# Down projection of a gated FFN, taken product by product over all channel pairs, with the block sums made earlier and kept in DRAM

## The chip, the cores and the metric

One core of one Trainium2 chip runs the whole kernel. The metric is device time in microseconds, the median of several runs. A profiled execution of the same program gives the trace; its times are microseconds from the start of the span unless marked ns. PE is TensorE's matmul, PEld its weight load, DVE VectorE, ACT ScalarE, POOL GpSimd, SP the engine whose queue issues most DMAs.

## What is computed

A decoder block on a sequence of 1024 tokens with 1024 channels, in float32: input projections, two kinds of token mixing, an output projection, and then a gated feed-forward part. The last part matters here:

```python
h = rmsnorm(x, norm2_g)
u = h @ w_ffn_up                      # 1024 x 5632
a, b = u[..., :D_FF], u[..., D_FF:]   # D_FF = 2816
a = causal_dwconv(a, ffn_conv_w, ffn_conv_b)
x = x + (jax.nn.silu(a) * b) @ w_ffn_down
return rmsnorm(x, norm_f_g)
```

## The kernel before

**Precision.** A float32 product is made of three matmuls (`mm3`, L206 to L209). Each operand is split (`split`, L194 to L196) into a high half, rounded by an ACT copy (L195), and a low half, the difference, made by DVE or, for the weights of the input projections, by POOL (L196).

**Seven products.** The up and the down projection use a Strassen-like scheme: both operands of a 2x2 block product are cut into four blocks, and seven block products take the place of eight. `left` (L1245) and `right` (L1261) make the sums and differences of blocks that a product needs, in place, on POOL mostly (`add` and `sub`, L1240 and L1243), and split them.

**Order.** The program is written in Python order, and a scheduler orders each engine's instructions by written order and by when it reckons them ready; the order in the trace is therefore not the written one everywhere. Tiles of one tag share a fixed number of buffers: `slab` and `sl2` (four each, 16 KB per partition), `raw` and `rw` (two each, for raw weights), `w4` and `op` (four each, operands), `f4` (four), and four PSUM tags of two banks.

**Early stage.** The values and gates of the mLSTM part are projected token tile by token tile (`vgates`, L283), then `gates()` (L312) makes the gate rows in two slabs, and 22 input projections follow (`project`, L400; `pweights`, L386, loads and splits one projection's weights into `w4` tiles). Each projection calls `tick()` twice (L377), which advances the generators in `active`, among them the mLSTM chunks.

**Up stage** (L1280 to L1389). For each of the 22 channel tiles f the loop loads four weight blocks, makes products 1 and 2 (`first_up`, L1322) and then 5, 6, 7, 3 and 4 (`rest_up`, L1341). A product is one PSUM bank, 12 matmuls. The convolution, the SiLU and the gating (`conv_up`, `gate_up`, L1330 and L1336) give the gated tile, two halves of 512 tokens, which are stored to `d_g` in DRAM.

**Down stage** (L1392 to L1500). Two channel tiles make a pair, 11 pairs in all. The pairs are taken in four groups of 2, 2, 3 and 4 (`GROUPS`). A pair's gated blocks and weight blocks are loaded once, 2 MB (`load_down`). Within a group all seven products are made one after the other (`prod_down`, L1428): it makes each pair's left and right sum, splits both, multiplies four token tiles into four PSUM banks, and adds each bank to a running tile in `X` (L1445, L1240). In the last group the running tiles are combined (`acc`) and rows are finished (`finish`, L1456): squares, root, scaling and the store of the output.

## Time and profile before

| | |
|---|---|
| median of 3 runs | 1388.04 us (1385.54 to 1392.6) |
| the profiled execution's own time | 1398.64 us |
| its span, first to last instruction | 1396.8 us |
| TensorE busy, of the span | 92% |
| DVE busy, of the span | 78% |
| ACT and POOL busy, of the span | 39% each |
| mean granted TensorE clock | 0.956 of full speed |

Busy shares are means over stages with different limits. The stages in the trace: gate projections and input projections to about 400 us, the token mixing to about 700, the up stage to 1133.5, the down stage to the end. A view of busy time over stretches of time shows which engine is full in which stage; the view of waits says what ended an idle time; the view of lines gives the mean duration of each kind of instruction.

### The profile page before, as it was taken

To read this page: it belongs to the slowest core of one execution; us is meant where nothing else is said; L and a number is where in the kernel's file an instruction comes from. 1 tells how busy PE (TensorE), PEld (TensorE's weight loads), DVE (VectorE), ACT (ScalarE), POOL (GpSimd) and SP (SyncE) were. 2 spreads that over 40 slices of the span, in tenths; PEclk is the share of its full clock that TensorE was granted. 3 is DMA by queue.
4 is the path that set the end of the run, shared out by engine and by line. 5 is a ranking of instruction groups with operands and counts; after the bars stand their busy time and mean duration, and the time that the engine had idled before them with its cause. 6 is when DMAs were issued, how large, how long until landed. Compare 5 with 4: busy or idle time off the path is not lost.

```text
span 1396.8 us, 20908 instructions
## 1 busy us (share of the span) xinstructions
PE 1285.8 (92%) x7814; PEld 1028.4 (74%) x7814; DVE 1084.9 (78%) x1777; ACT 540.4 (39%) x969; POOL 543.1 (39%) x379
## 2 busy tenths in 40 slices
PE   5999999888978889999989999999999999989794
PEld 5978777666767767677768888888888888768563
DVE  6376874898762786667599888787777878999998
ACT  6343334662211333223353434333333345434234
POOL 4102112534231334221464444333443365573971
PEclk9999999998995889899999999999999999999997
DMA  6111332365552664434324222222222293312003
GB/s 223 46 40 49 103 87 59 109 171 142 149 152 71 173 184 131 130 108 131 122 80 161 91 91 91 91 79 72 76 92 91 76 344 123 121 38 84 0 0 121
DMA packets 126549, 150.19 MB, mean 108 GB/s; under 512 B 49384, under 2 KB 88168, under 8 KB 126448
## 3 DMA queue, kind: packets, MB, share of 16 engines
q1 hardware_dynamic: 115568, 135.74, 30.9%
q10 hardware_dynamic: 10880, 13.11, 3.3%
q8 instruction: 62, 1.02, 0.3%
q14 instruction: 39, 0.32, 0.1%
HBM read 108.41 MB, written 40.40 MB: 107 GB/s over the span
## 4 chain that ended last, share of the span: by engine, by line
PE 59%; DVE 26%; issue 4%; ACT 4%; DMA 4%; POOL 2%; SPq 0%; DVEq 0%; ACTq 0%; POOLq 0%
PE ps L207 17%; PE ps L208 16%; PE ps L209 16%; DVE op L196 6%; DVE slab L196 2%; DVE slab L1240 2%; DVE sl L1240 2%; DVE slab L704 1%; PE ps L942 1%; DVE slab L702 1%; DMA d_x<-raw 1%; DVE w L273 1%; PE ps L1056 1%; DVE sv L606 1%; PE ps L1018 1%
## 5 line engine op out<-in xcount | busy, mean ns | idle before, releaser
L207 PE MATMUL ps<-sl,w 128*128 128x512 f32 x416 | 172.0, 414 | 0.0
L208 PE MATMUL ps<-sl,w 128*128 128x512 f32 x416 | 168.2, 404 | 1.2 <-POOL w L196 1.2
L209 PE MATMUL ps<-sl,w 128*128 128x512 f32 x416 | 168.4, 405 | 0.0
L207 PE MATMUL ps<-slab,op 128*128 128x512 f32 x388 | 156.4, 404 | 7.4 <-DVE slab L196 6.6
L1243 POOL TENSOR_TENSOR raw<-raw,rw 128x512 f32<-128x512 f32 x44 | 85.5, 1943 | 187.0 <-DVE op L196 181.0
L208 PE MATMUL ps<-slab,op 128*128 128x512 f32 x388 | 154.7, 399 | 2.8 <-DVE op L196 2.8
L209 PE MATMUL ps<-slab,op 128*128 128x512 f32 x388 | 154.8, 399 | 0.0
L196 POOL TENSOR_TENSOR w<-raw,w 128x1024 fp32r<-128x1024 f32 x22 | 54.1, 2459 | 209.1 <-ACT w L195 171.0
L207 PE MATMUL ps<-op,op 128*128 128x512 f32 x236 | 95.0, 402 | 20.2 <-ACT op L195 9.7
L207 PE MATMUL ps<-sl,op 128*128 128x512 f32 x264 | 104.4, 395 | 1.0 <-ACT op L195 1.0
L209 PE MATMUL ps<-sl,op 128*128 128x512 f32 x264 | 103.9, 394 | 0.0
L208 PE MATMUL ps<-sl,op 128*128 128x512 f32 x264 | 103.6, 392 | 0.3 <-DVE op L196 0.3
L195 ACT CAST op<-rw 128x512 fp32r<-128x512 f32 x79 | 48.8, 620 | 134.0 <-POOL rw L1240 51.0
L207 PEld LDWEIGHTS ps<-sl,w 128*128 128x128 f32 x416 | 80.1, 193 | 19.3 <-issue 1.8
L196 DVE TENSOR_TENSOR op<-rw,op 128x512 fp32r<-128x512 f32 x79 | 79.6, 1009 | 18.9 <-ACT op L195 16.4
L208 PEld LDWEIGHTS ps<-sl,w 128*128 128x128 f32 x416 | 80.6, 194 | 18.5 <-POOL w L196 1.7
L209 PE MATMUL ps<-op,op 128*128 128x512 f32 x236 | 93.9, 398 | 0.0
L207 PEld LDWEIGHTS ps<-slab,op 128*128 128x128 f32 x388 | 74.5, 192 | 26.1 <-DVE slab L196 8.3
L208 PE MATMUL ps<-op,op 128*128 128x512 f32 x236 | 93.6, 396 | 0.0
L209 PEld LDWEIGHTS ps<-sl,w 128*128 128x128 f32 x416 | 80.5, 193 | 17.5
L195 ACT CAST op<-raw 128x512 fp32r<-128x512 f32 x98 | 60.2, 619 | 85.7 <-PE ps L209 68.5
L208 PEld LDWEIGHTS ps<-slab,op 128*128 128x128 f32 x388 | 74.6, 192 | 20.5 <-DVE op L196 3.6
(343 smaller groups left out, 3114.2 us busy)
## 6 DMA issues: line engine op xcount, KB each, us to landing
raw<-in_wup_dram SPq DMA_DIRECT2D x23, 512.0 KB, 3.2
rw<-in_wup_dram SPq DMA_DIRECT2D x23, 512.0 KB, 3.8
raw<-in_wp_dram SPq DMA_DIRECT2D x22, 512.0 KB, 3.8
d_g<-f SPq DMA_DIRECT2D x44, 256.0 KB, 2.1
sl<-in_w_down_dram SPq DMA_DIRECT2D x10, 512.0 KB, 5.8
sl<-d_g SPq DMA_DIRECT2D x10, 512.0 KB, 5.1
w<-in_x_dram SPq DMA_DIRECT2D x8, 512.0 KB, 6.5
d_ar<-slab SPq DMA_DIRECT2D x8, 512.0 KB, 3.8
```

What stands on the lines that cost most here:

```text
L195: S.copy(out=h, in_=src)
L196: (leng or V).tensor_tensor(out=l, in0=src, in1=h.bitcast(F32), op=ALU.subtract)
L207: MM(out=ps, lhsT=ah, rhs=bl, start=start, stop=False)
L208: MM(out=ps, lhsT=al, rhs=bh, start=False, stop=False)
L209: MM(out=ps, lhsT=ah, rhs=bh, start=False, stop=stop)
L273: V.scalar_tensor_tensor(out=xt, in0=xt, scalar=ss, in1=g1, op0=ALU.mult, op1=ALU.mult)
L606: V.tensor_tensor_scan(out=e3, data0=rm, data1=sw, initial=0.0, op0=ALU.mult, op1=ALU.add)
L702: V.tensor_tensor(out=tv, in0=wv_[:, s_:s_ + 1, s_ + 1:32].broadcast_to([P, n, m]), in1=wv_[:, 0:n, s_:s_ + 1].broadcast_to([P, n, m]), op ...
L704: V.tensor_tensor(out=wv_[:, 0:n, s_ + 1:32], in0=wv_[:, 0:n, s_ + 1:32], in1=tv, op=ALU.add)
L942: MM(out=gps[e][:, q * P:(q + 1) * P], lhsT=bk[half[e], q, :], rhs=ar[half[e], q, :], start=True, stop=True)
L1240: eng.tensor_tensor(out=o, in0=a, in1=b, op=ALU.add)
L1243: eng.tensor_tensor(out=o, in0=a, in1=b, op=ALU.subtract)
```

## The change

In the down stage one product runs over all 11 pairs before the next begins, its sum staying in four PSUM banks. The order of products is 1, 6, 7, 5, 2, 3, 4. The sums of blocks are no longer made there. Those of the gated blocks are made in `gate_up`, in the up stage, mostly from running sums in a slab `GS`, and all seven left operands of a pair are stored to `d_go` (`keep`). Those of the weight blocks are made by `weight_sums`, a generator that is advanced three times among the gate projections and then once in each `tick()`: it loads a pair's four weight blocks, makes four differences, two on DVE and two on POOL, and stores all four to `d_w`. Each down step (a product of one pair) loads one left and one right operand (`load_down`), eight steps ahead, and splits them two steps ahead (`split_down`). The first eight loads are written before the last channel tile's `rest_up`, the first two splits before its product 4. The weights of the first input projection are loaded and split earlier, and `finish` has one activation less. The lines that go are the old down stage, L1392 to L1500.

```diff
-    d_g = dram.tile([NF, P, T], F32, name="d_g")
+    d_go = dram.tile([NP, 7, P, HALF], F32, name="d_go")
+    d_w = dram.tile([NP, P, 4, HALF], F32, name="d_w")
...
+    def ws_load(p):
+        if not ws_slab:
+            ws_slab.append(slab([P, 2, 4, HALF]))
+        wsums[p] = b = ws_slab[0][:, p % 2]
+        for q in range(2):
+            dma(out=b[:, 2 * q:2 * q + 2], in_=w_down[(2 * p + q) * P:(2 * p + q + 1) * P, :].rearrange("p (h t) -> p h t", h=2))
+
+    def ws_sum(p):
+        b11, b12, b21, b22 = (wsums[p][:, z] for z in range(4))
+        V.tensor_tensor(out=b11, in0=b12, in1=b11, op=ALU.subtract)
+        G.tensor_tensor(out=b12, in0=b22, in1=b12, op=ALU.subtract)
+        V.tensor_tensor(out=b22, in0=b22, in1=b11, op=ALU.subtract)
+        G.tensor_tensor(out=b21, in0=b21, in1=b22, op=ALU.subtract)
+
+    def ws_store(p):
+        dma(out=d_w[p], in_=wsums.pop(p))
+
+    def ws_jobs():
+        for i in range(3 * ((NP + 1) // 2) + 1):
+            for p in range(NP):
+                k = i - 3 * (p // 2) - p % 2
+                if 0 <= k < 3:
+                    (ws_load, ws_sum, ws_store)[k](p)
+            yield 1
...
     for tt in range(NT):
         vgates(1, tt)
+        if tt == 2:
+            PW["q0"] = pweights("q0")
+        if tt > 2 and tt % 2:
+            next(weight_sums)
...
     gates()
+    spawn(weight_sums)
...
+        GS = slab2([P, 8, HALF])
+        def keep(m, p, t):
+            dma(out=d_go[p, m - 1], in_=t)
+
         def gate_up(f, hf, b, t):
-            add_ = dict(out=t, in0=b, in1=t, op=ALU.mult)
-            V.tensor_tensor(**add_)
-            dma(out=d_g[f, :, HF[hf]], in_=t)
+            p, q = f // 2, f % 2
+            o = 4 * (p % 2)
+            if q == 0 and hf == 1:
+                V.tensor_tensor(out=GS[:, o], in0=b, in1=t, op=ALU.mult)
+                return
+            V.tensor_tensor(out=t, in0=b, in1=t, op=ALU.mult)
+            keep({(0, 0): 1, (1, 0): 2, (1, 1): 4}[q, hf], p, t)
+            if q == 0:
+                sub(GS[:, o + 1], t, GS[:, o])
+                keep(7, p, GS[:, o + 1])
+            elif hf == 1:
+                add(GS[:, o], GS[:, o], t)
+                keep(5, p, GS[:, o])
+                sub(GS[:, o + 2], t, GS[:, o + 1])
+                keep(6, p, GS[:, o + 2])
+            else:
+                sub(GS[:, o + 3], t, GS[:, o + 2])
+                keep(3, p, GS[:, o + 3])
...
+        MS = (1, 6, 7, 5, 2, 3, 4)
+        AHEAD, LAST, DEEP = 2, 4, 8
+        steps = [(m, p) for m in MS for p in range(NP)]
+        def load_down(i):
+            m, p = steps[i]
+            t = raws[i] = RAWD[i % DEEP // 4][:, i % 4]
+            dma(out=t[:, 0], in_=d_go[p, m - 1])
+            if m < 4:
+                r0 = (2 * p + (m > 1)) * P
+                dma(out=t[:, 1], in_=w_down[r0:r0 + P, HF[m == 3]])
+            else:
+                dma(out=t[:, 1], in_=d_w[p, :, {5: 0, 7: 1, 4: 2, 6: 3}[m]])
...
+        def op_down():
+            ring[0] += 1
+            z = ring[0] % 16
+            return op() if z % 2 else OPD[z // 8][:, z % 8 // 2]
+
+        def split_down(i):
+            if i >= len(steps):
+                return
+            ops[i] = []
+            for z in range(2):
+                o = op_down()
+                split(raws[i][:, z], o[:, 0], o[:, 1])
+                ops[i].append(o)
+            del raws[i]
+            if i + DEEP < len(steps):
+                load_down(i + DEEP)
+
+        def begin_down():
+            OPD.extend(slab2([P, 4, 2, HALF], F32R) for _ in range(2))
+            for i in range(AHEAD):
+                split_down(i)
...
+            if f < NF - 1:
+                rest_up(f)
+        RAWD.extend(slab([P, 4, 2, HALF]) for _ in range(2))
+        for i in range(DEEP):
+            load_down(i)
+        rest_up(NF - 1, begin_down)
...
         def finish(tt, n, ps):
+            mine = res(tt // 4, n, tt % 4)
+            add(mine, ps, mine, V)
...
+        def after(m, t, ps):
+            if m == 1:
+                S.copy(out=X1[:, t], in_=ps)
+                add(res(0, 0, t), res(0, 0, t), X1[:, t])
+            elif m == 6:
+                add(U2[:, t], ps, X1[:, t], V)
+                add(res(0, 1, t), res(0, 1, t), U2[:, t])
+            elif m == 7:
+                add(U3[:, t], ps, U2[:, t], V)
+                add(res(1, 1, t), res(1, 1, t), U3[:, t])
+                add(res(1, 0, t), res(1, 0, t), U3[:, t])
+            elif m == 5:
+                add(res(0, 1, t), ps, res(0, 1, t), V)
+                finish(4 + t, 1, ps)
+            else:
+                finish(*{2: (t, 0), 3: (t, 1), 4: (4 + t, 0)}[m], ps)
...
+        for k, m in enumerate(MS):
+            pst = [bank((dtag + 2 * (k % 2) + t % 2) % 4 + 1) for t in range(4)]
+            body = NP - LAST if k == len(MS) - 1 else NP - 1
+            for p in range(body):
+                split_down(k * NP + p + AHEAD)
...
+                for t in range(4):
+                    products(pst[t], t, k * NP + p)
+            for p in range(body, NP):
+                split_down(k * NP + p + AHEAD)
+            for t in range(4):
+                for p in range(body, NP):
+                    products(pst[t], t, k * NP + p)
+                after(m, t, pst[t])
```

`between` is called in `rest_up` ahead of product 4. At the third step of the first product the residual `d_x1` (4 MB, two slabs `XR`) and the final gain are loaded.

## Rows read from the trace of the kernel before

**Rows 1.** Windows, two stages: us, PE, PEld, DVE, ACT, POOL, clock, DMA share, GB/s.

```profile
760.00:1133.50 373.50, 373.50 (x1616) 303.61 (x1615) 298.86 (x431) 145.81 (x234) 149.31 (x82) 1.00 0.28 98
...
1133.50:1391.00 257.50, 226.08 (x925) 175.64 (x924) 243.67 (x286) 106.44 (x211) 153.88 (x96) 0.96 0.24 85
```

**Rows 2.** The same view, two stretches of 10 us in the down stage.

```profile
1310.00:1320.00 10.00, 4.72 (x16) 3.59 (x17) 9.97 (x7) 0.00 (x0) 9.84 (x7) 0.87 0.00 1
...
1360.00:1370.00 10.00, 2.75 (x12) 1.88 (x10) 10.00 (x13) 2.93 (x7) 5.45 (x4) 0.76 0.00 0
```

**Rows 3.** TensorE's waits in the down stage: us in total, times, longest.

```profile
PE ps L207 <- DVE op L196: 12.1, 15, 2.0
...
PE ps L207 <- ACT op L195: 9.7, 1, 9.7
```

**Rows 4.** Groups of instructions by line, down stage: busy us, mean ns, idle before.

```profile
L196 DVE TENSOR_TENSOR op<-sl,op 128x512 fp32r<-128x512 f32 x55 | 63.8, 1191 | 0.7 <-ACT op L195 0.7
...
L1240 DVE TENSOR_TENSOR sl<-ps,sl 128x512 f32<-128x512 f32 x56 | 34.9, 678 | 0.4 <-PE ps L209 0.4
...
L1243 POOL TENSOR_TENSOR sl<-sl 128x512 f32<-128x512 f32 x27 | 43.8, 1637 | 5.2 <-DVE op L196 3.6 <-DVE sl L1243 1.2
```

**Rows 5.** Groups of instructions by line and shape, up stage.

```profile
L1243 POOL TENSOR_TENSOR raw<-raw,rw 128x512 f32<-128x512 f32 x37 | 74.1, 2004 | 178.9 <-DVE op L196 177.4
...
L196 DVE TENSOR_TENSOR op<-rw,op 128x512 fp32r<-128x512 f32 x57 | 55.7, 977 | 18.0 <-ACT op L195 15.5
...
L196 DVE TENSOR_TENSOR op<-raw,op 128x512 fp32r<-128x512 f32 x74 | 51.7, 699 | 13.7 <-ACT op L195 13.5
...
L195 ACT CAST op<-raw 128x512 fp32r<-128x512 f32 x74 | 45.6, 620 | 57.1 <-PE ps L209 57.0
...
L415 DVE SCALAR_TENSOR_TENSOR f<-fa,pcs,f 128x510 f32<-128x510 f32 x20 | 31.4, 1572 | 0.7
...
L415 DVE SCALAR_TENSOR_TENSOR f<-f,pcs,f 128x510 f32<-128x510 f32 x19 | 14.1, 743 | 0.0
...
L1338 DVE TENSOR_TENSOR f<-fu,f 128x512 f32<-128x512 f32 x20 | 13.7, 684 | 0.0
```

**Rows 6.** Timeline, first matmul and last evacuation of the down stage: start us, us.

```profile
1133.55 0.39 PE L207 MATMUL ps<-op,op 128*128 128x512 f32 x1
...
1390.21 0.67 DVE L1240 TENSOR_TENSOR slab<-ps,slab 128x512 f32<-128x512 f32 x1
```

**Rows 7.** Busy time as rows 1; DMA issues, us to landing; SP timeline.

```profile
1145.00:1150.00 5.00, 5.00 (x23) 4.07 (x22) 3.96 (x5) 0.62 (x1) 4.92 (x3) 1.00 1.03 419
...
sl<-d_g SPq DMA_DIRECT2D x10, 512.0 KB, 5.1
...
d_g<-f SPq DMA_DIRECT2D x44, 256.0 KB, 2.1
...
1265.77 0.33 SPq L1400 DMA_DIRECT2D rw<-in_w_down_dram  x1
```

**Rows 8.** Timelines around 905 us, up stage: POOL, TensorE, DVE.

```profile
902.25 2.29 POOL L1243 TENSOR_TENSOR raw<-raw,rw 128x512 f32<-128x512 f32 x1 [10.39 <-DVE op L196]
...
905.87 0.40 PE L207 MATMUL ps<-sl,op 128*128 128x512 f32 x1
...
906.94 0.69 DVE L196 TENSOR_TENSOR op<-rw,op 128x512 fp32r<-128x512 f32 x1 [0.18 <-ACT op L195]
```

**Rows 9.** First projections: engines' busy time, a wait, timelines of POOL, ACT, DVE.

```profile
75.00:180.00 105.00, 100.91 (x525) 80.77 (x525) 80.95 (x205) 45.84 (x78) 16.51 (x9) 0.98 0.24 66
...
PE ps L365 <- ACT slab L360: 3.0, 1, 3.0
...
104.97 2.43 POOL L196 TENSOR_TENSOR w<-raw,w 128x1024 fp32r<-128x1024 f32 x1 [13.85 <-DMA sc<-d_sc]
...
114.72 1.05 ACT L195 CAST w<-raw 128x1024 fp32r<-128x1024 f32 x1
...
95.37 0.67 DVE L445 SCALAR_TENSOR_TENSOR slab<-sv,uv 128x512 f32<-128x512 f32 x1
```

More of the change, by code (lines that the diff above doesn't have):

```diff
@@ L25 @@
 HALF = 512
+NP = NF // 2
 C = 64
@@ L290, in vgates, with pweights @@
         V.tensor_tensor(out=gtm[:, g, tt, :], in0=ps[:, 256:260], in1=bb[:, 4 * g:4 * g + 4], op=ALU.add)
+    wsums = {}
+    ws_slab = []
+    def ws_load(p):
[19 more added lines that the diff above has]
+            yield 1
+    PW = {}
+    def pweights(name):
+        if name in PW:
+            return PW.pop(name)
+        raw = wload(wp[ORDER.index(name)])
+        h = w4((P, KT, P), F32R)
+        l = w4((P, KT, P), F32R)
+        split(raw, h, l, G)
+        return h, l
+    weight_sums = ws_jobs()
     norm1(0)
@@ L1362, in rest_up @@
             gate_up(f, 1, c22, t1_)
+            between()
             if f == 0:
@@ L1418, in block_kernel @@
-        SLOT.append([raw4((P, 2, HALF)), raw4((P, 2, HALF)), *(ff.tile([P, 2, HALF], F32, tag="rw", bufs=2, name=nm("rw"))
-                                                              for _ in range(2))])
-        for m, tt, n in ((2, 0, 0), (3, 0, 1), (4, 4, 0), (0, 4, 1)):
-            dma(out=X[m], in_=d_x1.rearrange("(t p) d -> p t d", p=P)[:, tt:tt + 4, HF[n]])
-        gf = [f4("fu", 3) for _ in range(2)]
-        for n in range(2):
-            dma(out=gf[n], in_=rows[2:3, HF[n]].broadcast_to([P, HALF]))
@@ new lines, in products @@
+        def products(ps, t, i):
+            p = steps[i][1]
+            a, b = ops[i]
+            ts = slice(t * P, (t + 1) * P)
+            mm3(ps, a[:, 0, ts], a[:, 1, ts], b[:, 0, :], b[:, 1, :], p == 0, p == NP - 1)
+        for k, m in enumerate(MS):
[3 more added lines that the diff above has]
+                split_down(k * NP + p + AHEAD)
+                if k == 0 and p == 2:
+                    for z in range(2):
+                        dma(out=XR[z], in_=d_x1.rearrange("(z t p) d -> z p t d", p=P, z=2)[z])
+                    for n in range(2):
+                        dma(out=gf[n], in_=rows[2:3, HF[n]].broadcast_to([P, HALF]))
+                for t in range(4):
[6 more added lines that the diff above has]
+                after(m, t, pst[t])
```

102 lines of the change are left out of this document (17 added, 85 removed).

## The prediction

> **What bounds the kernel now.** I read the windows by stage first. From 760 to 1133.5 us, the up projection, TensorE is busy for the whole stretch: 1616 matmuls in 373.5 us, so one matmul of 128x512 costs 0.2311 us when nothing is late. From 1133.5 to 1391 us, the down projection, it is busy for 226.1 of 257.5 us, and DVE for 243.7 [rows 1]. The finer windows show the worst places: in 1310 to 1320 and in 1360 to 1370 us TensorE works for 4.7 and 2.8 us of 10 while DVE works for all 10, and the mean granted clock of these windows is 0.87 and 0.76, where the full stage before has 1.00 [rows 1, 2]. The waits of TensorE in this stretch name the operand splits: DVE L196 ends 12.1 us of waiting and ACT L195 9.7, these two lines being the halves of a split [rows 3]. So in the down stage TensorE waits for operands, and the operands wait for DVE.
>
> Why DVE is full is in the lines of that stage: a split on DVE takes 1191 ns when its source is a `sl` tile, and an evacuation, which reads PSUM, takes 678 ns [rows 4]. In the up stage the same split takes 699 ns from `raw` and 977 ns from `rw`, and one tap of the convolution 1572 ns on one tile and 743 ns on another [rows 5]. What differs is POOL: it adds and subtracts 128x512 blocks at 1.6 to 2.0 us each, and DVE operations with two SBUF sources stretch beside it [rows 4, 5]. The down stage has 88 such block sums, most on POOL.
>
> The whole stage as a bill: its first matmul starts at 1133.55 and the last evacuation at 1390.21, so TensorE takes 256.7 us [rows 6]. Its matmuls number 7 products x 11 pairs x 4 tiles x 3 = 924, worth 924 x 0.2311 = 213.6 us. **43.1 us of the stage is waiting or slow clock.** Behind it come 6.6 us of finishing to the end of the span at 1396.8.
>
> **The change, part by part.**
>
> *Down stage.* The matmuls stay 924. Eight block sums per pair go (88), the 32 adds between partial results become 16 on POOL, and 112 evacuations become 28, because a product now stays in PSUM over all 11 pairs. The 154 splits stay. DVE then has 154 x 0.70 + 24 x 0.68 + 16 x 0.74 for the output scaling (priced as a tap) = 136 us, and ACT 154 x 0.62 plus copies and squares, about 115 us, both under 213.6; POOL has 16 adds of about 1.65 us [rows 4, 5]. So TensorE should set the pace. A product's evacuation lands on two PSUM tags while the next product fills the other two, so its 4 adds have a product's 30.5 us of cover; the next splits behind them on DVE have two steps, 5.5 us, against 4 x 0.68 + 2 x 0.70 = 4.1 us. Only the products that also finish rows are tighter (about 2.4 us of DVE per tile). I take 2 us lost in all; the ends are 0 and half of today's loss, 21.5 us, and the value is near the low end because the fuller up stage shows no loss at 80% DVE [rows 1].
>
> Each step now loads 512 KB, in two DMAs, instead of a pair loading 2 MB once for all seven products: 77 x 512 KB + 4 MB of x1 = 44.6 MB in 213.6 us, 209 GB/s. The trace moved 419 GB/s in 1145 to 1150, with TensorE busy throughout [rows 7]. The loads run 8 steps, 22 us, ahead, and a landing took 5.1 us for 512 KB [rows 7]. SP issues 154 loads at 0.33 us, 51 us of 214 [rows 7]. A load waits on SP for the splits of the step whose buffer it takes, and behind it wait only later loads. The x1 loads queue 4 MB before the loads of later steps, about 10 us, within those 22. I cost all of it at nothing. The first eight loads need the two slabs of products 1 and 2, free before the last 14 us of the up stage; the first two steps are split ahead of that stage's last product, so I see no gap at the seam.
>
> On transfers of this size a page speaks against the change: the Trainium skill ("DMA: Bandwidth & Descriptors", section "Measured (HBM→SBUF, 128 partitions, SWDGE, issued from GpSimd)") advises batches of 1 MiB and more, and its fit in "Anatomy of one DMA" gives some 2.6 us for 256 KB, an estimate from that page; 154 of those in a row would be 400 us. The trace disagrees as long as many are in flight, as the 419 GB/s show. That case is the last rival.
>
> *Up stage.* Per pair POOL gains 4 sums (44 in all) and SP 3 stores (77 of 256 KB in place of 44). POOL works 7.8 us per channel tile of 84 matmuls, 19.4 us, now [rows 1] and gets 2 x 1.9 more. DVE works 80% [rows 1]. The nearest rows for the contention are its stretched kinds: per channel tile three `rw` splits at +0.28 and one tap at +0.83 us make 1.7 us for 4 POOL operations, 0.43 each [rows 5], so DVE goes from 15.5 to 16.4 us of 19.4. If each sum held DVE for its whole 1.9 us it would reach 19.3, just under. Gates and conv buffers are now held until POOL has read them; what waits is the next tile's first ACT pass, with ACT casts and DVE splits queued behind. Their cover: the split of product 5 made at 906.94 is not for the product 5 that TensorE begins at 905.87, so it is for the one a channel tile later [rows 8]. I take 2 us, for the first tile, where the new slab has to wait for the old hidden blocks; below it is nothing (TensorE is at 100%, so no gain is possible), above some 12 us.
>
> *Early stage.* Eleven sums of weights, each a strict chain DVE, POOL, DVE, POOL, as each overwrites what the one before reads; 22 loads of 512 KB and 11 stores of 1 MB. Two of the sums fall into the gate projections, nine lie beside the first projections. There, in 75 to 180 us, DVE is busy for 81.0 of 105 us and TensorE for 100.9 [rows 9]. Added to DVE: 18 x 0.69 = 12.4 us and contention of 18 x 0.43 = 7.7 us, together 20 of 24 idle us. POOL also makes the low halves of the projection weights; that operation ends about 7 us before its projection (107.4 against 114.7, when the next cast shows the projection before it ended) [rows 9], which covers a POOL sum of 1.9 us and its wait. SP's weight loads queue behind loads that wait for a store two pairs back; they have a projection's 11 us. The slab that the sums hold makes the convolution's output wait for the gates' slabs, until about 99 us; before it started at 95.4 [rows 9]. TensorE already waits 3.0 us for the gates there [rows 9]. I take 5 us; ends: nothing (a gain could be 4 us at most, the idle there, and nothing added shortens a wait), and 16.5 us (below).
>
> **Sum**, against the profiled execution: 1398.64 - 43.1 + 2 + 2 + 5 = 1364.5, a gain of 34.1 us. That execution's time is 10.6 us above the median of the runs, 1388.04; the difference is carried over: **1353.9, said as 1354 us.** A measurement of this kernel can tell about 0.5%, 7 us, from no change.
>
> **The rivals.**
> (a) *The early sums are paid on TensorE.* If DVE stands through the first POOL sum of each chain, a sum holds it for 0.69 + 1.94 + 0.69 = 3.3 us: 81.0 + 9 x 3.3 + 7.7 = 118.5 against 105, 13.5 us over, and 3 more in the gates' chain. In place of my 5: **1366**. For it: the engines take instructions in order and the stage is TensorE-bound. Against: DVE's queue there has other work to put in between. Chance 0.15.
> (b) *The change does only half of what it says in the down stage:* operands only two steps ahead, and the finishing work of products 3 and 4 on DVE, keep half of the 43 us: 1354 + 21.5 - 2 = **1374**. For it: the last of today's losses stand around finishing too. Against: DVE falls to two thirds. Chance 0.15; in a third of it almost all of the loss stays, and the time is within 0.5% of before.
> (c) *Slower: POOL's order in the up stage.* As written, the last sum of a channel tile waits for product 4's gate and stands on POOL ahead of the two block sums for the next product 5. If POOL ran so, from the end of product 4: evacuation 0.68, gate 0.68, sum 2.0, two block sums 2.0 + 1.6, cast 0.62, split 0.98 = 8.6 us [rows 4, 5], against products 1 and 2 as cover, 24 x 0.2311 = 5.5 us. TensorE would lose 3.0 us on each of 21 tiles, 63 us: 1354 - 2 + 63 = **1415**. It decides against the change from 1.6 us per tile (34.1 / 21). Against it: the block sums now run a tile ahead of their use [rows 8], out of written order, and POOL had been idle for 10.4 us when it began them. Chance 0.07.
> (d) *The loads of the down stage do not overlap:* a lone 256 KB took 2.1 us [rows 7]; 154 in a row are 323 us, 110 above the matmuls: **1464**. Chance 0.02.
>
> **How the numbers follow.** The forecast keeps 0.61; its own range is 1346 to 1362 (the 9 us of costs down to nothing, or doubled). The range given, 1345 to 1379, adds (a) and most of (b) and leaves out (c), (d) and the part of (b) where the loss stays. Slower: (c) and (d), 0.09; the same: 0.05; faster 0.86.
>
> **What would show it.** Right: in the down stage TensorE within 2% of 0.231 us per matmul from its first to its last, splits at about 0.70 us, granted clock 1.00, no wait over 2 us except around the last two products; the up stage still full, with POOL near 60%. Wrong: idle TensorE before product 5 in the up stage released by POOL (c); TensorE between 75 and 200 us waiting for DVE or for a weight's POOL half (a); splits released by DMA in the down stage (d), or by finishing work (b).

## The result: 1.0 % faster, less than half of the gain forecast

Before, the runs beside the change had a median of 1387.72 us (1385.54 to 1392.6); the changed kernel has 1373.0 us (1369.5 to 1378.38). The ratio is 0.9897, with an interval of 0.987 to 0.9923: **14.7 us faster, where the forecast said 34.1.** The profiled execution of the changed kernel has a span of 1371.6 us and a time of 1373.39 us, close to the median.

The profile after, read as [rows 1]: the windows of the changed kernel for the same part of the up stage, its down stage, and two stretches of the early stage (us, then PE, PEld, DVE, ACT, POOL, granted clock, DMA share, GB/s).

```profile
760.00:1133.50 373.50, 373.47 (x1607) 301.42 (x1606) 298.85 (x422) 133.20 (x226) 195.21 (x116) 1.00 0.28 98
1147.50:1365.00 217.50, 214.82 (x926) 173.91 (x924) 140.06 (x210) 96.91 (x187) 32.50 (x19) 1.00 0.63 212
75.00:180.00 105.00, 90.54 (x450) 71.67 (x449) 83.44 (x182) 41.05 (x69) 32.89 (x21) 0.95 0.52 179
75.00:110.00 35.00, 25.01 (x110) 19.42 (x108) 24.83 (x39) 11.01 (x14) 8.76 (x7) 0.85 0.54 199
```

The down stage is what the forecast said: TensorE works for 214.8 of 217.5 us, DVE for 140 (136 forecast), POOL for 33, the granted clock is 1.00. The early stage is not: in 75 to 180 us TensorE does 450 matmuls in place of 525 [rows 9], and half of that is lost before 110 us. By then the whole delay is made: behind the gates the way to the token mixing takes 284.3 us, 286.0 before (the table below, e0). The kernel before, in the same 35 us of that last row:

```profile
75.00:110.00 35.00, 31.97 (x147) 25.87 (x146) 28.90 (x47) 16.98 (x26) 5.14 (x2) 0.95 0.19 56
```

The operations in the new down stage and up stage, as in [rows 4, 5]: lines by form, 1147.5 to 1365 us (the first), and 760 to 1133 us. L199 is now the DVE half of a split, L1284 and L1287 add and subtract, L458 is the tap.

```profile
L199 DVE TENSOR_TENSOR sl<-slab,sl 128x512 fp32r<-128x512 f32 x74 | 59.7, 807 | 2.3 <-ACT sl L198 2.2
...
L1287 POOL TENSOR_TENSOR raw<-raw,rw 128x512 f32<-128x512 f32 x38 | 81.4, 2142 | 162.4 <-DVE op L199 160.9
L199 DVE TENSOR_TENSOR op<-rw,op 128x512 fp32r<-128x512 f32 x56 | 60.7, 1084 | 66.0 <-ACT op L198 64.7
...
L1287 POOL TENSOR_TENSOR sl<-f,sl 128x512 f32<-128x512 f32 x29 | 45.3, 1562 | 0.8
```

A split in the down stage has fallen from 1191 to 807 ns (0.70 us forecast). In the up stage the stretched kinds grew by 11 and 7 % (977 to 1084, 2004 to 2142 ns), and POOL is busy for 195 of 373.5 us (52 %; the forecast said near 60).

**A ledger** along TensorE, from its timeline. The marks are the start of the last group of transposes of the gates' chain, of the first matmul of the token-mixing chain, of the first and of the last matmul of the up projection, and the end of the last matmul. The kernel before was profiled once more in the experiments (e0); its first profiled execution was long, and its token mixing is part of that: 311.4 us, against 305.8 in e0.

| kernel | gates | chain | up starts | up's last | end | span |
|---|---|---|---|---|---|---|
| before, first profile | 98.3 | 383.2 | 694.6 | 1133.3 | 1389.0 | 1396.8 |
| before, again (e0) | 97.8 | 383.8 | 689.7 | 1128.3 | 1382.6 | 1390.7 |
| after | 110.3 | 394.6 | 698.6 | 1147.4 | 1364.7 | 1371.6 |
| e1, sums on POOL | 104.0 | 400.5 | 700.3 | 1149.3 | 1369.0 | 1375.8 |
| e2, few loads | 109.6 | 395.5 | 698.2 | 1147.9 | 1365.1 | 1372.5 |
| e3, seam early | 109.4 | 393.8 | 696.2 | 1137.8 | 1357.2 | 1364.0 |
| e4, no weight sums | 97.9 | 380.7 | 686.6 | 1135.6 | 1353.1 | 1360.0 |
| e5, sums without transfers | 113.4 | 396.2 | 704.2 | 1152.6 | 1371.5 | 1378.5 |
| e6, sums after the gates | 96.9 | 407.3 | 707.8 | 1157.0 | 1374.6 | 1381.4 |
| e7, late split | 108.2 | 396.5 | 701.9 | 1143.9 | 1369.6 | 1376.4 |
| e8, e3 and no sums | 97.3 | 380.3 | 683.7 | 1124.2 | 1343.5 | 1350.5 |
| e9, sums in the down stage | 99.4 | 384.2 | 684.6 | 1124.5 | 1343.8 | 1351.2 |
| e10, sums on DVE | 101.9 | 388.3 | 689.9 | 1140.2 | 1357.7 | 1364.6 |
| e11, no block sums | 108.5 | 395.0 | 698.5 | 1137.2 | 1351.4 | 1358.2 |

After against e0: up to the chain +10.8, token mixing (up starts less chain) 304.0 against 305.8, -1.8; the up projection 448.8 against 438.7, +10.1; the down projection (end less up's last) 217.4 against 254.3, **-36.9**; the rest of the span -1.2. Together -19.0, and the spans differ by 19.1. So the down stage gave most of what was forecast (-41.1 by its own terms), and 20.9 us were given back in two places. The medians differ by 14.7; single executions of before lie up to 10 us apart, so some 4 us of the ledger belong to e0 itself.

**Place one, the gates.** TensorE waits 8.8 us at one place in 75 to 112 us, where the kernel before has one wait of 3.0 [rows 9], at later transposes; the granted clock of 75 to 110 us is 0.85 in place of 0.95. TensorE's and DVE's longest waits there, from the waits of the changed kernel:

```profile
PE ps L390 <- DVE gtm L385: 8.8, 1, 8.8
...
DVE slab L309 <- DMA slab<-in_w_down_dram: 6.9, 1, 6.9
...
DVE slab L311 <- POOL slab L310: 2.4, 1, 2.4
```

L390 are the gates' transposes, L385 ends the small operations ahead of them, L309 to L312 are the four differences of a weight sum. DVE's and then POOL's timeline of the changed kernel (start us, us) show how they come together:

```profile
76.31 0.69 DVE L311 TENSOR_TENSOR slab<-slab 128x512 f32<-128x512 f32 x1 [2.35 <-POOL slab L310]
...
79.16 0.18 DVE L379 TENSOR_SCALAR q<-q 128x32 f32<-128x32 f32 x1 [0.30 <-ACT q L378]
86.24 0.69 DVE L309 TENSOR_TENSOR slab<-slab 128x512 f32<-128x512 f32 x1 [6.89 <-DMA slab<-in_w_down_dram]
86.84 1.27 DVE L392 COPY slab<-ps 4x512 f32<-4x512 f32 x2
88.04 0.85 DVE L381 TENSOR_SCALAR q<-q 128x32 f32<-128x32 f32 x1
...
89.95 1.26 DVE L384 TENSOR_TENSOR q<-q 128x32 f32<-128x32 f32 x1
...
77.09 1.29 POOL L312 TENSOR_TENSOR slab<-slab 128x512 f32<-128x512 f32 x1 [0.81 <-DVE gtm L293]
...
89.91 1.26 POOL L312 TENSOR_TENSOR slab<-slab 128x512 f32<-128x512 f32 x1 [1.04 <-DVE slab L311]
```

From L379 to L381, two neighbours of the gates' chain, 8.9 us pass. Between them in DVE's queue stands a first difference, which waits 6.89 us for its load. It is the seventh pair's: the sums begin at 32.9 us, and six pairs are summed before the gates' chain begins at 77.9. SP's timeline of the changed kernel there:

```profile
75.06 3.66 SPq L315 DMA_DIRECT2D d_w<-slab  x2
78.93 6.59 SPq L304 DMA_DIRECT2D slab<-in_w_down_dram  x4
```

The stores are the fifth and the sixth pair's, the loads the seventh's and the eighth's. SP stands until 78.4 for the sixth pair's last difference on POOL, which had waited for DVE, which had waited for POOL. Then it waits 0.2 us more for a store of the slab to land (the seventh load takes the fifth pair's half), and only then issues the load.

**Place two, the seam.** TensorE's waits of the changed kernel from 1135 to 1156 us, and its windows there:

```profile
PE ps L211 <- DVE op L199: 3.3, 1, 3.3
PE ps L210 <- DVE fu L1284: 2.4, 1, 2.4
PE ps L210 <- ACT op L198: 2.2, 1, 2.2
```

```profile
1139.00:1153.00 14.00, 8.17 (x22) 5.68 (x22) 12.92 (x24) 10.56 (x19) 0.00 (x0) 0.76 1.02 366
```

That is 8.0 us of waiting and 22 matmuls at a mean granted clock of 0.76. 5.6 us of it are for splits; 2.4 are for L1284 on DVE, the evacuation of an up product. SP's timeline of the changed kernel before it:

```profile
1117.39 3.72 SPq L1384 DMA_DIRECT2D d_go<-sl  x3
1133.43 0.32 SPq L1384 DMA_DIRECT2D d_go<-f  x1
1134.81 0.32 SPq L1384 DMA_DIRECT2D d_go<-sl  x1
1135.22 0.38 SPq L1461 DMA_DIRECT2D slab<-d_go  x1
```

SP stands from 1121 to 1133.4 for a gate of the last tile but one, and to 1134.8 for a POOL sum. Behind these two stores come the first sixteen loads of the down stage, whose slab had been free since about 1125. DVE's idle time before the first split of a down operand (2.94 us) ends only at 1138.58, and the last split of the up stage (`rw`) stands behind it. ACT's timeline of the changed kernel, the first halves of these two splits:

```profile
1137.93 0.62 ACT L198 CAST op<-slab 128x512 fp32r<-128x512 f32 x1 [3.07 <-DMA slab<-d_go]
1138.45 0.61 ACT L198 CAST op<-rw 128x512 fp32r<-128x512 f32 x1
```

### The profile page after: what moved, and what is told of

The parts are those of the page before. It is cut to its first block, busy times and chain, and to the rows that moved or that the text cites. A ratio compares the mean times of both kernels' runs of the same rounds, so it can differ in the third digit from the quotient of the medians.

```text
span 1371.6 us, 21281 instructions
## 1 busy us (share of the span) xinstructions
PE 1272.5 (93%) x7814; PEld 1021.4 (74%) x7814; DVE 1005.8 (73%) x1723; ACT 524.9 (38%) x949; POOL 499.1 (36%) x357
## 4 chain that ended last, share of the span: by engine, by line
PE 38%; DVE 29%; POOL 13%; DMA 7%; ACT 7%; issue 6%; SPq 1%; DVEq 0%; ACTq 0%; POOLq 0%
PE ps L210 10%; PE ps L211 9%; PE ps L212 9%; DVE op L199 6%; POOL raw L1287 4%; DVE f L1284 3%; DVE fu L1284 3%; POOL rw L1287 2%; POOL sl L1287 2%; DVE f L458 2%; POOL rw L1284 2%; DVE slab L747 1%; PE ps L986 1%; ACT op L198 1%; DMA slab<-in_w_down_dram 1%
## 5 line engine op out<-in xcount | busy, mean ns | idle before, releaser
L210 PE MATMUL ps<-sl,op 128*128 128x512 f32 x572 | 227.1, 397 | 3.6 <-DVE fu L1284 2.4
L211 PE MATMUL ps<-sl,op 128*128 128x512 f32 x572 | 224.6, 393 | 1.4 <-DVE op L199 1.4
L212 PE MATMUL ps<-sl,op 128*128 128x512 f32 x572 | 225.2, 394 | 0.0
L1287 POOL TENSOR_TENSOR raw<-raw,rw 128x512 f32<-128x512 f32 x44 | 91.4, 2079 | 164.8 <-DVE op L199 160.9
L211 PE MATMUL ps<-slab,op 128*128 128x512 f32 x352 | 139.4, 396 | 6.3 <-DVE op L199 6.3
L210 PE MATMUL ps<-slab,op 128*128 128x512 f32 x352 | 140.1, 398 | 3.8 <-ACT op L198 3.0
L212 PE MATMUL ps<-slab,op 128*128 128x512 f32 x352 | 139.6, 396 | 0.0
L210 PEld LDWEIGHTS ps<-sl,op 128*128 128x128 f32 x572 | 107.5, 188 | 31.8 <-issue 3.4
L211 PEld LDWEIGHTS ps<-sl,op 128*128 128x128 f32 x572 | 108.0, 189 | 26.4 <-DVE op L199 2.2
L212 PEld LDWEIGHTS ps<-sl,op 128*128 128x128 f32 x572 | 107.7, 188 | 25.4
L199 DVE TENSOR_TENSOR op<-rw,op 128x512 fp32r<-128x512 f32 x68 | 72.0, 1060 | 66.8 <-ACT op L198 65.5
L199 DVE TENSOR_TENSOR op<-slab,op 128x512 fp32r<-128x512 f32 x77 | 61.4, 797 | 65.7 <-ACT op L198 65.7
L199 POOL TENSOR_TENSOR w<-raw,w 128x1024 fp32r<-128x1024 f32 x22 | 55.1, 2506 | 133.4 <-ACT w L198 129.8
L198 ACT CAST op<-rw 128x512 fp32r<-128x512 f32 x68 | 41.9, 619 | 156.7 <-POOL rw L1287 79.4
L198 ACT CAST op<-slab 128x512 fp32r<-128x512 f32 x77 | 47.8, 620 | 99.6 <-PE ps L212 54.4
L211 PEld LDWEIGHTS ps<-slab,op 128*128 128x128 f32 x352 | 66.8, 190 | 22.5 <-DVE op L199 7.2
```

What stands on the lines that cost most here:

```text
L198: S.copy(out=h, in_=src)
L199: (leng or V).tensor_tensor(out=l, in0=src, in1=h.bitcast(F32), op=ALU.subtract)
L210: MM(out=ps, lhsT=ah, rhs=bl, start=start, stop=False)
L211: MM(out=ps, lhsT=al, rhs=bh, start=False, stop=False)
L212: MM(out=ps, lhsT=ah, rhs=bh, start=False, stop=stop)
L1287: eng.tensor_tensor(out=o, in0=a, in1=b, op=ALU.subtract)
```

## The experiments

Times are medians, beside runs of before with medians of 1391.08 (e0 to e3), 1391.02 (e4 to e7) and 1390.61 us (e8 to e11). The marks are in the table above. e2, e4, e5, e8 and e11 leave out part of the computation, so their outputs are other numbers.

**e0, the kernel before once more.** No edit.

> The kernel before, unchanged, profiled a second time. Theory: the first profiled execution of it was some 10 us above the median because the token mixing ran long (383 to 695 us in the trace, 311 us), so a second one near 1388 us has that stretch at about 301 to 304 us, and the up and down stages unchanged (439 and 257 us). Rival: the 10 us lie in the up or down stage; then the down stage's 43 us of loss was overstated and reads about 33 us here.

1392.52 us, one run. The up stage takes 438.7 us in both profiles, the down stage 255.7 and now 254.3; token mixing is 5.6 us shorter. So 5.6 of the 6.1 us between the two spans lie there, and the forecast's loss in the down stage does not shrink to the rival's 33 us.

**e1, all four differences on POOL.**

```diff
-        V.tensor_tensor(out=b11, in0=b12, in1=b11, op=ALU.subtract)
+        G.tensor_tensor(out=b11, in0=b12, in1=b11, op=ALU.subtract)
...
-        V.tensor_tensor(out=b22, in0=b22, in1=b11, op=ALU.subtract)
+        G.tensor_tensor(out=b22, in0=b22, in1=b11, op=ALU.subtract)
```

> Of the changed kernel, all four differences of each weight pair on POOL, none on DVE. Theory (a DVE instruction stands at the head of its queue waiting for a weight load, and the gates' chain queues behind it): the 6.9 us wait of DVE for the load at 79 to 86 us is gone, the gates' last transposes come at about 99 us instead of 110.3, and the time falls by 9 to 12 us, to about 1362. Rival (the time of the early sums is contention and POOL work beside the gates): POOL has more to do, the transposes stay at 107 us or later, time within 3 us of 1373.

1383.49 us, ratio 0.9956 (0.9934 to 0.9978): slower than the change. The theory's 99 us for the gates and 1362 for the time are both missed: the gates' transposes come 6.3 us earlier, at 104.0, but the wait has moved. Waits of this kernel, 95 to 130 us:

```profile
DVE slab L488 <- DMA d_al<-slab: 7.6, 1, 7.6
...
PE ps L415 <- POOL slab L312: 5.7, 1, 5.7
```

The gates' own store `d_al` now stands on SP behind stores and loads of the slower sums, and by the profile TensorE waits for POOL. The chain starts 5.9 us later than in the change.

**e2, few loads.** Only two of the eleven pairs are loaded.

```diff
-        for q in range(2):
+        for q in range(2 if p < 2 else 0):
```

> Of the changed kernel, the weight sums load only the first two pairs; the other nine pairs are summed and stored from what stands in the slab (the product uses wrong weight sums). The sums' DVE and POOL work and their stores stay, the waits for loads go. Theory (the wait for the load is the cost): the gates' last transposes come at 99 to 102 us, DVE does not wait for a weight load after the first two, and the time is 8 to 11 us under the changed kernel's. Rival (DVE's and POOL's own work is the cost): the transposes stay at 107 us or later and the time within 3 us.

1374.34 us, one run; the gates at 109.6, no gain. DVE's longest waits of this kernel, 60 to 112 us:

```profile
DVE slab L311 <- POOL slab L310: 11.9, 7, 2.6
DVE slab L309 <- DMA d_w<-slab: 7.0, 5, 2.6
```

The wait for loads is replaced by one for the stores of the same slab, and DVE stands still longer for POOL. All eleven sums now run ahead of the gates or beside them (32.5 to 88.3 us). So the load alone is not the cause; between the hop and the stores this run doesn't decide.

**e3, the seam early.** Products 1 and 2 of the last channel tile and the first eight loads of the down stage are written ahead of the rest of the tile before.

```diff
-            if f > 2:
+            if 2 < f < NF - 1:
                 first_up(f)
-            if f < NF - 1:
+            if f < NF - 2:
                 rest_up(f)
+        first_up(NF - 1)
         RAWD.extend(slab([P, 4, 2, HALF]) for _ in range(2))
         for i in range(DEEP):
             load_down(i)
+        rest_up(NF - 2)
         rest_up(NF - 1, begin_down)
```

> Of the changed kernel, products 1 and 2 of the last channel tile and the first eight down loads are written before the rest of the tile before, so the loads stand on SP ahead of that tile's stores. Theory (the loads were late because they queued on SP behind a store that waits for a gate, and the last up split queued on ACT behind a down split that waits for the load): TensorE's three waits at the seam, 8.0 us, and the half-speed matmuls after them, 2 us, go; time about 1363, the down stage unchanged at 217 us less 2. Rival (DVE and POOL are too full around the last tiles): the waits at the seam stay within 3 us of 8.0, released by DVE with no DMA behind.

1367.27 us (four runs, 1355.71 to 1368.87), ratio 0.9819 (0.9771 to 0.9868). From the start of the up projection to its last matmul 441.6 us, where the change has 448.8; the first load is issued at 1117.93, not 1135.22. TensorE's waits of this kernel from 1110 to 1160 us:

```profile
PE ps L210 <- DVE f L1284: 2.2, 1, 2.2
PE ps L210 <- DVE fu L1284: 1.0, 1, 1.0
```

So 3.2 of the 8.0 us stay, and both are for evacuations of up products, which stand on DVE among the down splits; from up's last matmul to the end it is 219.3 us (217.4 in the change). From the start of up to the end the kernel takes 661.0 us in place of 666.1: the place of the loads on SP's queue is worth 5.1 us. The other part of the span's -7.6 us lies ahead of the up stage, where nothing was changed.

**e4, no weight sums.** Neither made nor loaded; the down stage takes a block of `w_down` in their place.

```diff
-        if tt > 2 and tt % 2:
-            next(weight_sums)
...
-    spawn(weight_sums)
...
-                dma(out=t[:, 1], in_=d_w[p, :, {5: 0, 7: 1, 4: 2, 6: 3}[m]])
+                dma(out=t[:, 1], in_=w_down[2 * p * P:(2 * p + 1) * P, HF[m % 2]])
```

> Of the changed kernel, the weight sums, their loads and their stores are left out; the right operands that need them are loaded from the weights as they are (wrong products, same transfers and matmuls in the down stage). All theories: this is the whole price of the early sums. If the early part costs what the traces say, the gates' last transposes come at 98 to 99 us, the first matmul of the token mixing's chain at 383 to 385 us instead of 394.6, and the time falls to 1360 to 1364. If the 12 us come from the rest of the change (the slab held, the order of the engines), the transposes stay near 110 us.

1361.81 us, one run; span 1360.0, **11.6 us below the change: the price of the early sums**, as far as two single executions tell it. The gates are back at 97.9, the chain at 380.7; the seam is as in the change (449.0 us of up projection).

**e5, the sums without their transfers.** As e2 and e4's last line, with one store left.

```diff
-        dma(out=d_w[p], in_=wsums.pop(p))
+        if p == NP - 1:
+            dma(out=d_w[p], in_=wsums.pop(p))
```

> Of the changed kernel, the eleven sums are made with all their DVE and POOL instructions, but only the first two pairs are loaded and only the last is stored (wrong right operands, loaded from the weights as they are). Theory (waits for transfers at the head of DVE's and SP's queues are the price): the gates' last transposes come within 2 us of the run without sums, time within 2 us of it. Rival (DVE's and POOL's own work is the price): the transposes stay 6 us or more later than there.

1380.26 us, one run. With nothing to wait for, all eleven sums were packed ahead, into 33 to 82 us; DVE's longest wait of this kind in 40 to 75 us:

```profile
DVE slab L311 <- POOL slab L310: 6.0, 4, 2.5
```

The first input projection starts at 89.5 in place of 75.7, the gates come at 113.4. Transfers alone are not the cause: the chain DVE, POOL, DVE, POOL costs by itself. The sums also stretch each other here: L309, DVE's first difference, takes 1673 ns in the median, 684 in the change.

**e6, the sums after the gates.** No steps among the gate projections; the generator is started with the projection `q1`.

```diff
-        if tt > 2 and tt % 2:
-            next(weight_sums)
...
-    spawn(weight_sums)
     for name in ORDER[:-IN_CHAIN]:
+        if name == "q1":
+            spawn(weight_sums)
```

> Of the changed kernel, the weight sums start after the first input projection and not among the gate projections, so their slab comes free only behind the gates and no sum can stand ahead of the gates' chain on DVE. Theory: the gates' last transposes come at 98 to 100 us; the sums' transfers now share SP's queue with the chunks' and the projections' loads, so part comes back by 383 us: the chain starts at 386 to 392, time 1364 to 1370. Rival (the sums cost their DVE work wherever they stand): the transposes come early, but the chain starts at 394 us or later and the time stays within 3 us of 1373.

1389.19 us, ratio 0.9988 (0.9965 to 1.0011): the gain is gone. The gates come at 96.9, but the chain starts at 407.3. Theory and rival had 1364 to 1376 us; both are missed. TensorE's longest wait of this kernel, 100 to 180 us, and its windows from 140 to 160 us, then those of e4, which makes no sums:

```profile
PE ps L508 <- DVE bt L541: 5.0, 1, 5.0
...
140.00:160.00 20.00, 15.04 (x68) 11.29 (x66) 15.79 (x48) 7.26 (x15) 9.32 (x6) 0.74 0.68 259
...
140.00:160.00 20.00, 18.95 (x117) 14.74 (x117) 16.39 (x62) 9.13 (x19) 3.38 (x3) 1.00 0.34 84
```

`bt` belongs to a chunk of the mLSTM part, which runs beside the projections. There the same sums cost more than among the gates: TensorE waits for the chunks, and the granted clock falls to 0.74. Which queue holds the chunks up is not shown.

**e7, the first down splits later.** `between()` is called after product 4's gate, not before product 4.

```diff
-            between()
...
             gate_up(f, 0, u, t0)
+            between()
```

> Of the changed kernel, the first two down splits are written after the last up product instead of before it. Theory (the last up split queued on ACT behind a down split that waits for its load): the wait of 2.2 us and most of the 3.3 us before and in product 4 go, but the loads are as late as they were, so TensorE waits once at the first down step, 2 to 5 us; 2 to 4 us gained at the seam. Rival (the loads alone set the seam): the sum of the waits at the seam stays at 8 us.

1378.22 us, one run. Up's last matmul comes 442.1 us after its first (448.8 in the change), but from there to the end it is 225.7 us (217.4). The theory's gain of 2 to 4 us is not there. TensorE now waits once for long, at the first down step; that wait, and DVE's timeline of this kernel before it:

```profile
PE ps L210 <- DVE f L1284: 8.8, 1, 8.8
...
1147.44 0.69 DVE L199 TENSOR_TENSOR sl<-slab,sl 128x512 fp32r<-128x512 f32 x1 [0.27 <-ACT sl L198]
...
1152.25 0.68 DVE L1284 TENSOR_TENSOR f<-ps,fu 128x512 f32<-128x512 f32 x1
```

With the first of these rows the operands of the first two down steps are split, by 1148.1. The first down matmul comes at 1153.08, when the evacuation is through. So the wait has moved behind the seam, and there it is for a place on DVE: evacuations of up products stand behind further down splits.

**e8, e3 and e4 together.** Both edits, of which the first and the last lines are:

```diff
-            if f > 2:
+            if 2 < f < NF - 1:
...
-                dma(out=t[:, 1], in_=d_w[p, :, {5: 0, 7: 1, 4: 2, 6: 3}[m]])
+                dma(out=t[:, 1], in_=w_down[2 * p * P:(2 * p + 1) * P, HF[m % 2]])
```

> The seam edit (first loads of the down stage issued two tiles earlier) together with no weight sums: the right operands of products 4 to 7 are then blocks of w_down itself, so four of the seven products are not the reference's. Theory (two separate prices, 11.6 us early and 7.6 us at the seam, that add up): gates' last transposes at 97.9, first chain matmul at 380.7, from up start to last up matmul 441.6, span 1371.6 - 11.6 - 7.6 = 1352.4, time 1354. Rival (they share a wait, one hides behind the other): span 1357 or more. Other rival (a third price still hides beside them): below 1349.

1355.61 us, ratio 0.9753 (0.9724 to 0.9782); span 1350.5. The two prices add up: by spans 21.1 us against 11.6 + 7.6 = 19.2, by times 17.4 against 11.2 + 5.7 = 16.9. That the time is near the forecast's 1354 confirms little: the forecast had 5 us for early sums, which are not made here.

**e9, the sums in the down stage.** e3's edit, no early sums, and the order of products 1, 2, 3, 7, 6, 5, 4.

```diff
+                bs = [w_down[(2 * p + z // 2) * P:(2 * p + z // 2 + 1) * P, HF[z % 2]] for z in range(4)]
+                x, y = {7: (bs[3], bs[1]), 6: (d_w[p, :, 0], bs[0]), 5: (bs[1], bs[0]), 4: (bs[2], d_w[p, :, 1])}[m]
+                dma(out=t[:, 1], in_=x)
+                dma(out=XU[0][:, i % 8], in_=y)
+        def sum_down(i):
+            if i < len(steps) and steps[i][0] > 3:
+                r = raws[i][:, 1]
+                (add if steps[i][0] == 6 else sub)(r, r, XU[0][:, i % 8], G)
+        def store_down(i):
+            if i < len(steps) and steps[i][0] in (7, 6):
+                dma(out=d_w[steps[i][1], :, 7 - steps[i][0]], in_=raws[i][:, 1])
...
             del raws[i]
+            sum_down(i + 3)
+            store_down(i + 2)
...
+                add(res(0, 1, t), res(0, 1, t), X1[:, t])
+            elif m == 3:
+                add(res(0, 1, t), ps, res(0, 1, t), V)
+            elif m == 7:
+                add(U3[:, t], ps, X1[:, t], V)
+            elif m == 6:
+                add(res(0, 1, t), ps, res(0, 1, t), V)
+                add(U3[:, t], ps, U3[:, t], V)
```

> Weight sums out of the early stage and into the down stage itself, and the seam edit: the products go in the order 1, 2, 3, 7, 6, 5, 4, and in the last four each step loads a second block beside its right operand and GpSimd makes one sum, three steps ahead; products 7 and 6 store theirs for the products after them. 44 sums of 1.3 to 2.0 us on GpSimd in 4 x 31.1 = 124 us, where it was busy 19 %, and 44 more loads and 22 stores of 256 KB, 17 MB in 124 us beside the 23 MB of before, some 325 GB/s. Theory (the sums are dear only where in-order queues have work behind them that TensorE needs soon): early marks as without sums (97.9, 380.7), seam as with the edit, down stage 217 + 1 to 3 us, time 1355 to 1358. Rival (GpSimd or the transfers fall behind one step's 2.8 us): the last four products take over 3.1 us per step, +13 us or more, time 1368 or more.

1357.59 us (1353.07 to 1362.19), ratio 0.976 (0.9735 to 0.9786): **faster than both kernels, 33 us below before.** Its windows, the down stage and 75 to 110 us, and the down stage of e8, which makes no sums:

```profile
1124.50:1344.00 219.50, 216.15 (x926) 174.50 (x924) 168.19 (x216) 96.90 (x186) 97.38 (x63) 0.99 0.81 281
...
75.00:110.00 35.00, 31.97 (x149) 25.96 (x148) 27.85 (x45) 17.36 (x27) 5.14 (x2) 0.95 0.17 45
...
1124.20:1343.50 219.30, 216.14 (x926) 174.67 (x924) 139.39 (x211) 96.86 (x186) 33.41 (x19) 0.99 0.60 202
```

The 44 sums and 66 more transfers triple POOL's work in the down stage and lift DVE's from 139 to 168 us, and the stage takes 219.3 us with them and without them. (The 1.9 us over the change come with e3's edit; e3 has 219.3 too.) The early stage is that of the kernel before. The same sums cost 11.6 us there and here none that the traces show; the times of e9 and e8 differ by 2.0 us, and their ranges overlap.

**e10, all four differences on DVE.**

```diff
-        G.tensor_tensor(out=b12, in0=b22, in1=b12, op=ALU.subtract)
+        V.tensor_tensor(out=b12, in0=b22, in1=b12, op=ALU.subtract)
...
-        G.tensor_tensor(out=b21, in0=b21, in1=b22, op=ALU.subtract)
+        V.tensor_tensor(out=b21, in0=b21, in1=b22, op=ALU.subtract)
```

> All four differences of a pair on VectorE, none on GpSimd; transfers and places as in the change. Theory (the hop between two engines holds VectorE: it stands at its head until GpSimd's sum is through): gates' last transposes at 104 or earlier (110.3 in the change, 97.9 without sums), span 1365 or less. Rival (the wait is for the loads and stores of the slab, whichever engine sums): gates at 109 to 111, span 1370 to 1374. Other rival (22 more instructions of 0.7 us fill VectorE): later than 112.

1366.35 us, one run; span 1364.6, 7.0 below the change; the gates at 101.9. DVE's timeline of this kernel, at the same place as the changed kernel's above, and a row of SP's:

```profile
74.13 0.69 DVE L312 TENSOR_TENSOR slab<-slab 128x512 f32<-128x512 f32 x1
...
79.01 0.18 DVE L379 TENSOR_SCALAR q<-q 128x32 f32<-128x32 f32 x1 [0.29 <-ACT q L378]
79.33 1.28 DVE L392 COPY slab<-ps 4x512 f32<-4x512 f32 x2
81.59 0.69 DVE L309 TENSOR_TENSOR slab<-slab 128x512 f32<-128x512 f32 x1 [0.99 <-DMA slab<-in_w_down_dram]
82.20 0.18 DVE L381 TENSOR_SCALAR q<-q 128x32 f32<-128x32 f32 x1
...
83.03 0.19 DVE L384 TENSOR_TENSOR q<-q 128x32 f32<-128x32 f32 x1
...
75.81 4.37 SPq L304 DMA_DIRECT2D slab<-in_w_down_dram  x4
```

The sixth pair's last difference is through at 74.8 in place of 78.4, SP issues the seventh's load at 75.81 in place of 78.93, and DVE's wait for it is 0.99 us in place of 6.89; from L379 to L381 it is 3.2 us in place of 8.9. Without POOL the gates come 8.4 of 12.4 us earlier, though DVE does 22 more operations now. Not all of the 8.4 is the hop between two engines: L381 and L384 no longer run beside a POOL difference, 0.18 and 0.19 us in place of 0.85 and 1.26, which is 1.7 us, and two copies of the gates' chain (L392) now stand ahead of the sum. The other 4 us, against no sums, remain.

**e11, no block sums in the up stage.** The gates are stored in their place.

```diff
-                sub(GS[:, o + 1], t, GS[:, o])
-                keep(7, p, GS[:, o + 1])
+                keep(7, p, GS[:, o])
...
-                add(GS[:, o], GS[:, o], t)
                 keep(5, p, GS[:, o])
-                sub(GS[:, o + 2], t, GS[:, o + 1])
-                keep(6, p, GS[:, o + 2])
+                keep(6, p, t)
...
-                sub(GS[:, o + 3], t, GS[:, o + 2])
-                keep(3, p, GS[:, o + 3])
+                keep(3, p, t)
```

> Leaves out the four block sums of each pair of gate tiles in the up stage; what is stored in their place is the gate itself, as often and as large, so products 3, 5, 6 and 7 of the down projection are of other numbers. Theory (the seam comes from the order on the DMA queue, loads behind stores that wait for the last gates; the sums only cost the up stage's steady part 2.2 us): from up start to last up matmul 448.8 - 2.2 = 446 to 447. Rival (GpSimd's sums are what the stores and so the loads wait for): 441 or less.

1360.02 us, one run; span 1358.2. The up projection takes 438.7 us, as in the kernel before, and the down stage 214.2 in place of 217.4: from the start of up to the end 13.2 us less. TensorE does not wait at the seam at all. So not only the 2 us of the steady part are gone, the seam's 8 and the slow clock around them are too. The theory put down there, that the sums cost only the steady part, falls. SP's timeline of this kernel:

```profile
1120.15 0.32 SPq L1384 DMA_DIRECT2D d_go<-sl  x1
1120.75 0.32 SPq L1384 DMA_DIRECT2D d_go<-f  x1
1121.16 0.41 SPq L1457 DMA_DIRECT2D slab<-d_go  x1
```

Without the sums the stores are through at 1121 and the loads follow at once, 14 us earlier, ahead of the stores that waited in the change. That joins with e3 in part: two quite different edits bring the loads to 1118 and 1121 us, but e3 gives 5.1 us and keeps waits for evacuations, and this run closes the seam whole. What e11 doesn't separate is how much of the shift is POOL's work and how much the new order of the queue that came with it.

## Why the prediction was wrong

*Down stage: right.* Forecast 43.1 us of waiting, of which 2 stay. Measured against the second profile of before it fell by 36.9; in the changed kernel the 924 matmuls take 216.9 us from the first to the last, 3.3 over 213.6, and 2.4 of that is the last wait of the seam. The 43.1 was a little too large: it ran to the start of the last evacuation, and the last matmul ends 1.2 us before that (41.9 us; 40.4 in e0). DVE fell to 140 us, TensorE waits for no split behind the seam, the granted clock is 1.00. Rival (b), half of the gain, is refuted; that its 1374 us is 1 us from the measured time is luck. So is (d) refuted: 256 KB loads landed in 3.3 to 4.9 us (medians) and overlapped, 212 GB/s over the stage, 281 in e9. The Trainium skill ("DMA: Bandwidth & Descriptors", section "Measured (HBM→SBUF, 128 partitions, SWDGE, issued from GpSimd)") advises batches of 1 MiB and more. The trace shows no need of them here: with many loads of 256 KB in flight, none held TensorE up from 1155 to 1365 us.

*Early stage: the first step that failed.* "I take 5 us" measured 11.6 (e4), within the ends given, 0 and 16.5. Of the rivals (a) is nearest, DVE held through POOL's sum, at a chance of 0.15; but that direct wait is 2.4 us at the gates, and the larger one, 6.9 us for a load that SP issues late for POOL's sake, nobody had priced. The place was not (a)'s either. The forecast counted DVE's busy time over 75 to 180 us, and only (a) had 3 us for the gates' chain. The sums beside the projections cost 1 to 3 us: from the gates to the low-rank projections (L639) 132.3 us pass in the change, 131.1 before and 129.4 in e4. Nearly the whole price stands in the gates' chain, where TensorE soon has nothing else to do and a chain of small DVE operations is the path. There the count of busy time doesn't show it; what a queue's head waits for does: POOL's sum, then the store, then the load. The step "two of the sums fall into the gate projections, nine lie beside the first projections" was read off the written order; in the trace six pairs are summed before the gates' chain, two within it and three beside the projections (109.9, 123.7 and 138.0 us), so most stand ahead of operations written before them. "DVE's queue there has other work to put in between", the reason against (a), had it backwards: the sums were put in between the gates' operations.

*Seam: the second step that failed.* "So I see no gap at the seam", costed at nothing, was 8.0 us of waits, with a mean granted clock of 0.76 around them. The forecast looked at when the slabs come free (about 1125, as it turned out, well ahead) and not at what stands ahead of the loads on SP's queue: stores that wait for the last gates and for POOL. The place of the loads alone gave 5.1 us back (e3). The rest is waits for evacuations that stand on DVE among the down splits (e3, e7), which the forecast did not look at; without the block sums they are gone too (e11).

*Up stage: right in size, wrong in kind.* Forecast 2 us for the first tile. The steady part lost about as much, evenly from the sixth tile on: 1607 matmuls against 1616 in 373.5 us, 9 x 0.2311 = 2.1 us; the first five tiles took 108.5 us as before, so the loss put on the first tile did not occur and the size is luck. Without the block sums (e11) the rate is that of before. Rival (c), 63 us, did not occur: TensorE's waits show none in 760 to 1133 us. DVE's busy time did not move (298.86 to 298.85).

*The sum.* In the forecast's own terms: down -41.1, early +5, up and seam +2, total -34.1. In the second pair of profiles: down -36.9, early with token mixing +9.0, up and seam +10.1, ends -1.2, total -19.0; by the medians -14.7. (The forecast's own range, 9 us either way, should read 1345 to 1363; nothing hangs on it.) Two unpriced queues, SP's and DVE's, make most of the miss; e8, without early sums and with the loads ahead, is at 1355.6, and e9, which keeps the computation whole, at 1357.6.

What stays open: why token mixing took 311.4 us in the first profile of before and 300 to 308 in others of the same code; what of the seam in e11 is POOL's work; and which queue made the sums so dear in e6.

## What to carry to other kernels

Work moved to a "free" place is priced by what the head of each in-order queue will wait for there, and by who is queued behind; busy time alone did not tell it: the same sums cost 11.6 us beside the gates, where DVE was busy for 25 of 35 us, and no time that the traces show in a stage where POOL and DVE had steady, deep-buffered work and the operands were loaded eight steps ahead. At the border of two stages look at the DMA queue: the next stage's first loads belong ahead of the last stores that wait for results, and the evacuations that free the next stage's banks ahead of its splits. The first was tried here (e3), the second was not. A chain that hops between two engines on one buffer holds the buffer, its store and the next load for its whole length; on DVE alone it was shorter even though DVE was the busier engine (e10).

## What had not been expected of the hardware

Two small DVE operations stood until POOL's instruction was through. In the changed kernel L384, on 128x32, runs from 89.95 to 91.21 beside a POOL difference from 89.91 to 91.17: 1.26 us, where it takes 0.19 in e10, whose POOL is idle there. The Trainium skill ("SBUF — State Buffer", section "Who interferes with whom") says that a DVE instruction with two SBUF inputs contends with a GpSimd instruction that reads SBUF; this pair agrees, 1.26 against 0.19 us. L381, with one SBUF input, did the same: from 88.04 to 88.89 beside a POOL difference that ended at 88.86, 0.85 us in place of 0.18 in e10.

A TensorE that is shown as fully busy can still be slower: in the up stage the windows show 373.47 of 373.5 us busy with nine matmuls fewer than before. Only the count shows it.
